# Gated MLP of a decoder trunk: chunk 3 moved from plain products to seven block products, and the opening's splits reordered

## The chip, the cores and the metric

The kernel runs on one core of a Trainium2 chip. The metric is device time in microseconds of one execution; lower is better. A core has TensorE (PE, matrix products into PSUM), VectorE (DVE), ScalarE (ACT), GpSimd (POOL) and SyncE (SP), which issues most loads. POOL issues the transfers that add into their destination.

## The reference, cut to what matters

Two layers. Layer 0 begins with a mixer of a gated recurrence and pooling, layer 1 with a convolution module; both then have cross-attention and a gated MLP, and a norm ends the trunk. All is float32, with 512 tokens of width 1024. The MLP:

```python
def conv_ffn(x, norm, w_up, dw_w, dw_b, w_down):
    h = rms_norm(x, norm) @ w_up                       # 1024 -> 2 x 3072
    g = causal_dwconv(h[..., :D_FF], dw_w, dw_b)       # width 3
    u = h[..., D_FF:]
    return (jax.nn.gelu(g) * u) @ w_down
```

## The kernel before, in words

Activations lie transposed: partitions hold channels, the 512 columns are tokens. Every operand of a product is split into a high half (a copy rounded to fp32r, on ScalarE) and a low half (the rest, by a subtraction on VectorE), and a product is three matmuls, high-high, high-low and low-high (`mm3`, lines 183 to 187).

The 3072 channels of the gate and of the value branch are 24 chunks of 128 each (`CF`). Chunk c of the gate and chunk c of the value make a chunk pair. A layer's `ffn` (line 813) does the pairs in two ways.

The first four (`GC` = 4) are plain, in `opening` (line 938). `start(i)` (944) is one product of 128 weight columns with all 512 tokens: 8 blocks x 3 = 24 matmuls of 512 columns. Even i is a gate, odd i a value. `fetch(i)` (951) loads the piece of weights for it, 512 KB, and makes its high half; `w[-1].low()` makes the low half. `gate(c)` (955) is a generator in four steps: multiply by the norm's factor and scale for the convolution; two shifted multiply-adds; GELU; multiply by the norm's factor again. `values(c)` (971) multiplies by the value and makes the high half of the result, `close(c)` (976) the low half.

The other pairs are units (`unit(c)`, 867). Gate and value chunk, each in two halves of input channels, are seen as a 2 x 2 block matrix, the tokens' halves as another, and the product is made with seven block products in place of eight, after Strassen and Winograd: seven times 4 blocks x 3 = 12 matmuls of 256 columns, and seven additions of half width (line 170) plus one copy (880). The weights are four blocks (a11 and a12 are the gate chunk's two halves, `z` and a22 the value chunk's) and four sums of them (s1 to s4). A sum is not computed on an engine: a transfer on POOL's queue adds one block to another in SBUF, in place, issued right behind the low half that was the last reader of the old content (`Blocks.low`, line 797 and on):

```python
            if name == "a11":
                G.dma_start(self.r, self.z, accum_op=ALU.add)     # line 803, gives s3
            elif name == "a22" and not self.ring:
                G.dma_start(self.z, self.a22, accum_op=ALU.add)   # line 805, gives s1
            elif name == "s3":
                G.dma_start(self.r, self.a22, accum_op=ALU.add)   # line 807, gives s2
            elif name == "s2":
                G.dma_start(self.r, self.a12, accum_op=ALU.add)   # line 811, gives s4
```

So a11, s3, s2 and s4 of one pair are a chain through one buffer, and a22 and s1 another; each split (high at line 793, low at 800) has to wait for the transfer in front of it. The tokens' sums are made by `Seven.sums(k)` for k = 0 to 3 (727); the last, `sums(3)`, stands in the opening.

A unit c also has work for its neighbours: the splits of pair c + 1 and the first of pair c + 2, and two down products (`Down`, 816) of 12 matmuls of 512 columns each, of which the second runs over into the next unit's additions. Down products begin with chunk 4, when the first group of four chunks is complete. In a unit the order of products is a11, a12, s2, s3, then the first down product, s1, s4, a22, then the second.

Within `tc.manual_schedule(engines=ORDERED)` the queues of PE, ACT, DVE and POOL run in program order, so a waiting instruction holds all behind it. SP's order is chosen by the scheduler: a load goes out when its buffer is free. There are 3 buffers for raw weights, 4 each for their wide high and low halves, 4 for the small blocks a12 and a22, and 5 PSUM banks for the products.

Of the kernel before, what the change touches and what calls it, by code (L numbers as in the profile page):

```python
# [15 lines left out]
P = 128  # L16
# [8 lines left out]
CF = D_FF // P  # L25
NG = 6
GC = CF // NG
EPS = 1e-6
AHEAD = 100
PAIRED = (0, 4, 1, 5, 2, 6, 3, 7)  # L30
# [30 lines left out]
def trunk(ctx: ExitStack, tc: tile.TileContext, I: dict, out: list):  # L61
# [751 lines left out]
    def ffn(layer, norm, nxt, seven):  # L813
# [19 lines left out]
                if self.g == NG - 1:  # L833
                    nxt.feed(n)

        pairs = {c: Blocks(I["wpair"][layer * (CF - GC) + c - GC]) for c in range(GC, CF)}
        downs = {c: Down(*divmod(c - GC, GC)) for c in range(GC, CF + GC)}

        def high(c, name):
            if c in pairs:  # L840
                pairs[c].high(name)

        def low(c, name):
            if c in pairs:
                pairs[c].low(name)

        def gating(c, f, g, ps, u3):
# [19 lines left out]
        def unit(c):  # L867

            nonlocal left, due

            def m(j, block):
                return seven.product(main_ps()[:, :M], pairs[c].w[block], j)

            f, g, u, v = tmp_f(), tmp_f(), tmp_f(), tmp_f()
            m1, u2, u3, u4 = u[:, :M], u[:, M:], v[:, :M], v[:, M:]
            ps = m(seven.B11, "a11")
            next(left, None)
            A.activation(m1, ps, AF.Copy)  # L880
            high(c + 1, "s3")
            high(c + 1, "a22")
            if due:
                due()
            next(left, None)

            ps = m(seven.B21, "a12")
            low(c + 1, "s3")
            low(c + 1, "a22")
            add(g[:, :M], ps, m1)  # L890
            next(left, None)

            ps = m(seven.T2, "s2")
            high(c, "s4")
            high(c + 2, "a11")
            high(c + 1, "a12")
            add(u2, ps, m1)
            low(c, "s4")

            ps = m(seven.T3, "s3")  # L900
            low(c + 2, "a11")
            low(c + 1, "a12")
            add(u3, ps, u2)
            if c in downs:
                due = downs[c].out(0, aux_ps())
            if c + 1 in downs:
                downs[c + 1].w.high()
            if c + 3 in pairs:
                pairs[c + 3].load()
            if c + 2 in pairs:  # L910
                pairs[c + 2].load_second()
            if c + 1 in downs:
                downs[c + 1].w.low()
            if c + 2 in downs and c + 2 <= CF:
                downs[c + 2].load()
            if due:
                due()

            ps = m(seven.T1, "s1")
            high(c + 1, "s2")  # L920
            add(u4, ps, u2)
            add(f[:, M:], ps, u3)

            ps = m(seven.B22, "s4")
            low(c + 1, "s2")
            high(c + 1, "s1")
            add(g[:, M:], ps, u4)

            ps = m(seven.T4, "a22")
            left = gating(c, f, g, ps, u3)  # L930
            next(left)
            low(c + 1, "s1")
            next(left)
            if c in downs:
                due = downs[c].out(1, aux_ps())


        def opening():


            nonlocal left, due
            norm.r, ps, y = None, {}, [None] * GC

            def start(i):

                ps[i] = main_ps()
                x = w.pop(0)
                for k in range(C):
                    mm3(ps[i], blk(x, k * P), norm.x[k], k == 0, k == C - 1)

            def fetch(i):
                w.append(Piece(I["wup"][(layer * 2 + i % 2) * GC + i // 2]))
                w[-1].high()

            def gate(c):
                g = tmp_f()
                V.tensor_tensor(g, ps.pop(2 * c), norm.r, op=ALU.mult)
                y[c] = tmp_f()
                dw = lambda j: col("f_dw_w", (layer * 3 + j) * CF + c)
                A.activation(y[c], g, AF.Identity, scale=dw(2), bias=col("f_dw_b", layer * CF + c))  # L960
                yield
                for s in (1, 2):
                    V.scalar_tensor_tensor(
                        y[c][:, s:], g[:, : T - s], dw(2 - s), y[c][:, s:], op0=ALU.mult, op1=ALU.add
                    )
                yield
                A.activation(y[c], y[c], AF.Gelu_apprx_tanh)
                yield
                V.tensor_tensor(y[c], y[c], norm.r, op=ALU.mult)

            def values(c):
                V.tensor_tensor(y[c], ps.pop(2 * c + 1), y[c], op=ALU.mult)
                ys[c] = act_r(), act_r()
                A.activation(ys[c][0], y[c], AF.Copy)

            def close(c):
                V.tensor_tensor(ys[c][1], y[c], ys[c][0].bitcast(F32), op=ALU.subtract)

            ss = split(norm.ss)
            start(0)  # L980
            fetch(2)
            w[-1].low()
            for name in ("a11", "a22", "a12"):
                high(first, name)
                low(first, name)
            norm.r = scale_of(mean_of(ss))
            Norm.due = None

            start(1)
            fetch(3)  # L990
            w[-1].low()
            g = gate(0)
            next(g)
            high(first, "s3")
            high(first, "s1")
            next(g)
            low(first, "s3")
            next(g)
            low(first, "s1")
            next(g, None)  # L1000

            start(2)
            fetch(4)
            values(0)
            w[-1].low()
            close(0)

            start(3)
            fetch(5)
            w[-1].low()  # L1010
            g = gate(1)
            next(g)
            high(first, "s2")
            next(g)
            low(first, "s2")
            next(g)
            next(g, None)

            start(4)
            fetch(6)  # L1020
            w[-1].low()
            values(1)
            t = seven.sums(3)
            next(t)
            close(1)
            next(t, None)

            start(5)
            fetch(7)
            w[-1].low()  # L1030
            g = gate(2)
            next(g)
            next(g)
            next(g)
            next(g, None)

            start(6)
            pairs[second].load()
            pairs[second].load_second()
            downs[first].load()  # L1040
            values(2)
            close(2)
            high(second, "a11")

            start(7)
            downs[first].w.high()
            g = gate(3)
            next(g)
            low(second, "a11")
            next(g)  # L1050
            downs[first].w.low()
            next(g)
            downs[second].load()
            pairs[second + 1].load()
            next(g, None)

            def rest():
                values(3)
                yield
                close(3)  # L1060

            left, due = rest(), None

        left, due = None, None
        first, second = GC, GC + 1
        with tc.high_priority(AHEAD):
            w = [Piece(I["wup"][(layer * 2 + k) * GC]) for k in range(2)]
            for x in w:
                x.high()
                x.low()  # L1070
# [2 lines left out]
            pairs[first].load_second()  # L1073
        with tc.manual_schedule(engines=ORDERED):
            opening()
            for c in range(GC, CF):
                unit(c)
            due()
            for _ in left:
                pass  # L1080
# [572 lines left out]
    with tc.manual_schedule(engines=ORDERED | {mybir.EngineType.SP}):  # L1653
# [20 lines left out]
        ps = [[mm_ps(), mm_ps()] for _ in range(2)]  # L1674
# [28 lines left out]
        w = [Piece(I["wk"][0])]  # L1703
# [61 lines left out]
def _cols(w):  # L1765

    k, n = w.shape
    return w.reshape(k // P, P, n // P, P).transpose(2, 1, 0, 3).reshape(n // P, P, k)
# [9 lines left out]
def _fours(g, v):  # L1778

    return np.concatenate([g[:, :, :T], v[:, :, :T], v[:, :, T:], g[:, :, T:]], axis=2)  # L1780


def _layout(inputs):
    a = {k: np.asarray(v) for k, v in inputs.items()}
    params = []
    w = np.concatenate([np.zeros((1, D), np.float32), a["c_dw_w"][0]])[::-1].reshape(8, 4, C, 4, 32)[:, ::-1]
    a["c_dw_w"] = a["c_dw_w"][:, :TAPS]
    a["c_dw_pe"] = w.transpose(2, 0, 3, 4, 1)
    for name, width in _PARAMS:
# [4 lines left out]
    up = a["f_w_up"]  # L1794
# [17 lines left out]
        "wk": np.concatenate([_cols(w) for w in a["xa_wk"]]),  # L1812
        "wv": wv,
        "wo": np.concatenate([_cols(w) for w in a["xa_wo"]]),
        "wup": np.concatenate([_cols(w[:, at : at + GC * P]) for w in up for at in (0, CF * P)]),
        "wpair": np.concatenate([_fours(w[GC:CF], w[CF + GC :]) for w in map(_cols, up)]),
        "final_norm": np.broadcast_to(a["final_norm"], (P, D)),
        "wdown": np.concatenate([_pairs(w, GC).reshape(-1, P, D) for w in a["f_w_down"]]),
    }
# [19 lines left out]
```

## Time and profile before

| | before |
|---|---|
| median of 3 runs | 1432.36 us |
| lowest, highest | 1431.59, 1434.14 us |
| the profiled execution | 1434.17 us |
| its span | 1432.3 us |
| PE, DVE, ACT, POOL busy | 99%, 82%, 56%, 21% |
| opening of the MLP, layer 0, start(0) to the first unit | 356.1 to 400.1 us |
| one unit with its two down products | 15.55 us |

The profile is of one execution. The busy share counts an engine's instructions, recorded lengths united; matmuls are pipelined, so a matmul's recorded length is longer than the step to the next. Lines of the profile name the engine, the kernel's line, the tiles written and read, the count, and in a timeline the start in us from the beginning of the span, with the idle time in front and what ended it in brackets.

### The profile page before, as it was taken

The numbers are of one execution on the slowest core, as the hardware profiler recorded it, in microseconds if no ns is written. First come the engines' busy times: TensorE is split into PE (matmuls) and PEld (weight loads), VectorE is DVE, ScalarE is ACT, GpSimd is POOL, SyncE is SP. The second block draws the span as 40 slices with busy tenths as digits, with TensorE's granted clock in tenths as the row PEclk, the third lists the DMA queues.
The fourth block names the chain that finished last, engine by engine and source line by source line (L and its number), as shares of the span: only waits on it lengthen the run. The fifth ranks groups of instructions, "written<-read, shape, count | busy, mean of one in ns | idle before, by whom it ended". The sixth has DMA issues, their size and how long they took to land.

```text
span 1432.3 us, 22644 instructions
## 1 busy us (share of the span) xinstructions
PE 1419.6 (99%) x8504; PEld 1257.3 (88%) x8504; DVE 1176.7 (82%) x1955; ACT 798.2 (56%) x1321; POOL 304.4 (21%) x317
## 2 busy tenths in 40 slices
PE   9999999999999999999999999999999999999997
PEld 7888888998899999999988777899889999999997
DVE  6987776778788888888888997978778888888885
ACT  7678754666544444544565547767655444444434
POOL 0001310200021221222008992010001222222201
PEclk9999999999999999999999999999999999999999
DMA  8523232542557777777432464345244876787741
GB/s 292 198 81 99 93 118 81 118 111 89 158 136 169 162 182 165 163 173 173 136 123 89 118 167 143 107 87 147 87 129 121 178 179 157 171 184 159 162 126 59
DMA packets 77517, 200.11 MB, mean 140 GB/s; under 512 B 8672, under 2 KB 9952, under 8 KB 77408
## 3 DMA queue, kind: packets, MB, share of 16 engines
q1 hardware_dynamic: 50624, 150.15, 33.6%
q0 software_dynamic: 26496, 48.25, 20.5%
q8 instruction: 67, 1.10, 0.3%
q14 instruction: 42, 0.34, 0.1%
q10 hardware_dynamic: 288, 0.27, 0.1%
HBM read 145.16 MB, written 2.10 MB: 103 GB/s over the span
## 4 chain that ended last, share of the span: by engine, by line
PE 91%; DVE 3%; POOL 2%; DMA 2%; ACT 1%; issue 1%; SPq 0%; POOLq 0%; ACTq 0%; DVEq 0%
PE mm L186 22%; PE mm L185 22%; PE mm L187 22%; PE aux L185 7%; PE aux L186 7%; PE aux L187 7%; PE mm L456 2%; DMA raw<-in_wv 1%; DVE wlo L166 1%; POOL actf L1443 1%; PE aux L529 0%; ACT whi L165 0%; POOL act L166 0%; POOL tmp L1264 0%; DMA raw<-in_win 0%
## 5 line engine op out<-in xcount | busy, mean ns | idle before, releaser
L186 PE MATMUL mm<-act,whi 128*128 128x512 f32 (+2 forms) x1093 | 385.1, 352 | 0.6 <-DVE act L180 0.5
L185 PE MATMUL mm<-act,whi 128*128 128x512 f32 (+2 forms) x1093 | 384.6, 353 | 0.1
L187 PE MATMUL mm<-act,wlo 128*128 128x512 f32 (+2 forms) x1093 | 384.6, 352 | 0.0
L186 PEld LDWEIGHTS mm<-act,whi 128*128 128x128 f32 x1093 | 206.6, 189 | 30.3 <-DVE act L166 1.0
L185 PEld LDWEIGHTS mm<-act,whi 128*128 128x128 f32 x1093 | 206.4, 189 | 30.0 <-ACT tmp L1442 0.8
L187 PEld LDWEIGHTS mm<-act,wlo 128*128 128x128 f32 x1093 | 206.6, 189 | 27.0
L793 ACT ACTIVATE bigr<-raw 128x512 fp32r<-128x512 f32 x160 | 100.7, 630 | 156.7 <-DMA raw<-wa 64.3
L187 PE MATMUL mm<-bigr,bigr 128*128 128x256 f32 x640 | 181.1, 283 | 0.0
L186 PE MATMUL mm<-bigr,bigr 128*128 128x256 f32 x640 | 181.1, 283 | 0.0
L185 PE MATMUL mm<-bigr,bigr 128*128 128x256 f32 x640 | 180.9, 283 | 0.0
L170 DVE TENSOR_TENSOR tmp<-mm,tmp 128x256 f32<-128x256 f32 x322 | 131.2, 420 | 34.7 <-PE mm L187 28.3
L185 PE MATMUL aux<-act,whi 128*128 128x512 f32 x399 | 156.3, 392 | 0.0
L186 PE MATMUL aux<-act,whi 128*128 128x512 f32 x399 | 156.2, 391 | 0.0
L187 PE MATMUL aux<-act,wlo 128*128 128x512 f32 x399 | 155.2, 389 | 0.0
L165 ACT ACTIVATE whi<-raw 128x1024 fp32r<-128x1024 f32 (+1 forms) x95 | 96.6, 1021 | 85.5 <-PE mm L186 44.5
L800 DVE TENSOR_TENSOR bigr<-raw,bigr 128x512 fp32r<-128x512 f32 x160 | 110.0, 688 | 32.4 <-ACT bigr L793 30.4
L186 PEld LDWEIGHTS mm<-bigr,bigr 128*128 128x128 f32 x640 | 122.7, 192 | 1.6
L185 PEld LDWEIGHTS mm<-bigr,bigr 128*128 128x128 f32 x640 | 122.7, 192 | 1.6
L187 PEld LDWEIGHTS mm<-bigr,bigr 128*128 128x128 f32 x640 | 122.7, 192 | 0.0
L803 POOL DMA_DIRECT2D raw<-raw x46 | 39.8, 866 | 350.8 <-DVE wlo L800 303.9
L166 DVE TENSOR_TENSOR wlo<-raw,whi 128x1024 fp32r<-128x1024 f32 (+1 forms) x75 | 90.7, 1212 | 19.7 <-ACT whi L165 19.5
L807 POOL DMA_DIRECT2D raw<-wa x46 | 39.7, 864 | 303.2 <-DVE bigr L800 253.6
(341 smaller groups left out, 3013.4 us busy)
## 6 DMA issues: line engine op xcount, KB each, us to landing
raw<-wa POOLq DMA_DIRECT2D x138, 256.0 KB, 4.4
big<-in_wdown SPq DMA_DIRECT2D x42, 512.0 KB, 6.7
wa<-in_wpair SPq DMA_DIRECT2D x80, 256.0 KB, 3.4
raw<-in_wpair SPq DMA_DIRECT2D x40, 512.0 KB, 5.7
raw<-in_pw SPq DMA_DIRECT2D x24, 512.0 KB, 3.5
raw<-raw POOLq DMA_DIRECT2D x46, 256.0 KB, 7.3
raw<-in_win SPq DMA_DIRECT2D x20, 512.0 KB, 3.4
raw<-in_wk SPq DMA_DIRECT2D x16, 512.0 KB, 3.7
```

The lines of the kernel that those rows point to most:

```text
L165: A.activation(hi, src, AF.Copy)
L166: fetched[1] = (eng or V).tensor_tensor(lo, src, hi.bitcast(F32), op=ALU.subtract)
L170: V.tensor_tensor(out, a, b, op=ALU.add)
L185: PE.matmul(ps, wh, xh, start=first, stop=False)
L186: PE.matmul(ps, wh, xl, start=False, stop=False)
L187: PE.matmul(ps, wl, xh, start=False, stop=last)
L456: PE.matmul(p, m[j], x, start=k == 0 and j == 0 and x is hi, stop=k == C - 1 and x is lo)
L793: A.activation(self.w[name][0], self.block(name), AF.Copy)
L800: V.tensor_tensor(lo, self.block(name), hi.bitcast(F32), op=ALU.subtract)
L803: G.dma_start(self.r, self.z, accum_op=ALU.add)
L807: G.dma_start(self.r, self.a22, accum_op=ALU.add)
L1443: G.tensor_tensor(z[:, s:], z[:, s:], f[:, s:], op=ALU.add)
```

## The change

`PLAIN = 3` takes the place of `GC` wherever the number of plain pairs is meant, so that chunks 0 to 2 stay plain and chunk 3 becomes the first unit, in both layers. `GC` stays the number of chunks in a down group; unit 3 has no down products. The opening then holds start(0) to start(5). Its splits are put in another order: each split of a block sum (s3, s1, s2) of the first unit's pair comes some steps behind the transfer that makes the sum. The splits of a11, a22 and a12 of the second pair, chunk 4, are also made in the opening; the set `early` keeps the unit from making them again. `sums(3)` moves from start(4) to start(3), and the low half of a piece often behind the first step of a gate. The host's layout of the two weight arrays follows.

```diff
+PLAIN = 3
...
-        pairs = {c: Blocks(I["wpair"][layer * (CF - GC) + c - GC]) for c in range(GC, CF)}
+        pairs = {c: Blocks(I["wpair"][layer * (CF - PLAIN) + c - PLAIN]) for c in range(PLAIN, CF)}
...
+        early = set()
+
         def high(c, name):
-            if c in pairs:
+            if c in pairs and (c, name) not in early:
                 pairs[c].high(name)
...
-            if c + 1 in downs:
+            if c >= GC and c + 1 in downs:
                 downs[c + 1].w.high()
...
             start(1)
             fetch(3)
-            w[-1].low()
             g = gate(0)
             next(g)
+            w[-1].low()
             high(first, "s3")
-            high(first, "s1")
+            fetch(4)
+            next(g)
             next(g)
             low(first, "s3")
-            next(g)
-            low(first, "s1")
+            w[-1].low()
             next(g, None)
 
             start(2)
-            fetch(4)
             values(0)
-            w[-1].low()
+            fetch(5)
             close(0)
+            high(first, "s1")
 
             start(3)
-            fetch(5)
-            w[-1].low()
+            downs[GC].load()
+            pairs[second].load_second()
             g = gate(1)
             next(g)
-            high(first, "s2")
+            w[-1].low()
+            low(first, "s1")
+            pairs[second].load()
             next(g)
-            low(first, "s2")
-            next(g)
-            next(g, None)
-
-            start(4)
-            fetch(6)
-            w[-1].low()
-            values(1)
             t = seven.sums(3)
             next(t)
+            next(g)
+            next(t, None)
+            high(second, "a11")
+            next(g, None)
+
+            start(4)
+            values(1)
+            low(second, "a11")
+            early.add((second, "a11"))
+            high(first, "s2")
             close(1)
-            next(t, None)
+            low(first, "s2")
 
             start(5)
-            fetch(7)
-            w[-1].low()
+            downs[GC].w.high()
             g = gate(2)
             next(g)
+            high(second, "a22")
+            downs[GC].w.low()
             next(g)
             next(g)
+            high(second, "a12")
+            low(second, "a22")
             next(g, None)
-
-            start(6)
...
-            start(7)
...
+            low(second, "a12")
+            early.update(((second, "a22"), (second, "a12")))
             pairs[second + 1].load()
-            next(g, None)
...
-        first, second = GC, GC + 1
+        first, second = PLAIN, PLAIN + 1
...
-            for c in range(GC, CF):
+            for c in range(PLAIN, CF):
                 unit(c)
```

More of the change, by code (lines that the diff above doesn't have):

```diff
@@ L834, in sum @@
                     nxt.feed(n)
-        pairs = {c: Blocks(I["wpair"][layer * (CF - GC) + c - GC]) for c in range(GC, CF)}
+        pairs = {c: Blocks(I["wpair"][layer * (CF - PLAIN) + c - PLAIN]) for c in range(PLAIN, CF)}
         downs = {c: Down(*divmod(c - GC, GC)) for c in range(GC, CF + GC)}
+        early = set()
         def high(c, name):
-            if c in pairs:
+            if c in pairs and (c, name) not in early:
                 pairs[c].high(name)
         def low(c, name):
-            if c in pairs:
+            if c in pairs and (c, name) not in early:
                 pairs[c].low(name)
@@ L911, in unit @@
                 pairs[c + 2].load_second()
-            if c + 1 in downs:
+            if c >= GC and c + 1 in downs:
                 downs[c + 1].w.low()
@@ L941, in opening @@
             nonlocal left, due
-            norm.r, ps, y = None, {}, [None] * GC
+            norm.r, ps, y = None, {}, [None] * PLAIN
             def start(i):
@@ L951, in fetch @@
             def fetch(i):
-                w.append(Piece(I["wup"][(layer * 2 + i % 2) * GC + i // 2]))
+                w.append(Piece(I["wup"][(layer * 2 + i % 2) * PLAIN + i // 2]))
                 w[-1].high()
@@ L1008, in opening @@
             start(3)
-            fetch(5)
-            w[-1].low()
+            downs[GC].load()
+            pairs[second].load_second()
             g = gate(1)
             next(g)
-            high(first, "s2")
+            w[-1].low()
+            low(first, "s1")
+            pairs[second].load()
             next(g)
-            low(first, "s2")
+            t = seven.sums(3)
+            next(t)
             next(g)
+            next(t, None)
+            high(second, "a11")
             next(g, None)
@@ L1019, in opening @@
             start(4)
-            fetch(6)
-            w[-1].low()
             values(1)
-            t = seven.sums(3)
-            next(t)
+            low(second, "a11")
+            early.add((second, "a11"))
+            high(first, "s2")
             close(1)
-            next(t, None)
+            low(first, "s2")
             start(5)
-            fetch(7)
-            w[-1].low()
+            downs[GC].w.high()
             g = gate(2)
             next(g)
+            high(second, "a22")
@@ L1033, in opening @@
+            downs[GC].w.low()
             next(g)
             next(g)
+            high(second, "a12")
+            low(second, "a22")
             next(g, None)
-            start(6)
[L1038 to L1043, printed above, removed]
-            start(7)
-            downs[first].w.high()
-            g = gate(3)
-            next(g)
-            low(second, "a11")
@@ L1050, in opening @@
[L1050 to L1053, printed above, removed]
+            low(second, "a12")
+            early.update(((second, "a22"), (second, "a12")))
             pairs[second + 1].load()
-            next(g, None)
             def rest():
-                values(3)
+                values(2)
                 yield
-                close(3)
+                close(2)
             left, due = rest(), None
         left, due = None, None
-        first, second = GC, GC + 1
+        first, second = PLAIN, PLAIN + 1
@@ L1066, in ffn @@
         with tc.high_priority(AHEAD):
-            w = [Piece(I["wup"][(layer * 2 + k) * GC]) for k in range(2)]
+            w = [Piece(I["wup"][(layer * 2 + k) * PLAIN]) for k in range(2)]
             for x in w:
@@ L1814, in _layout @@
         "wo": np.concatenate([_cols(w) for w in a["xa_wo"]]),
-        "wup": np.concatenate([_cols(w[:, at : at + GC * P]) for w in up for at in (0, CF * P)]),
-        "wpair": np.concatenate([_fours(w[GC:CF], w[CF + GC :]) for w in map(_cols, up)]),
+        "wup": np.concatenate([_cols(w[:, at : at + PLAIN * P]) for w in up for at in (0, CF * P)]),
+        "wpair": np.concatenate([_fours(w[PLAIN:CF], w[CF + PLAIN :]) for w in map(_cols, up)]),
         "final_norm": np.broadcast_to(a["final_norm"], (P, D)),
```

## The prediction

> **What bounds the kernel now.** I read the page's head and chain first, then the waits of TensorE, then stretches of the gated MLP.
>
> ```profile
> span 1432.3 us, 22644 instructions
> PE 1419.6 (99%) x8504; PEld 1257.3 (88%) x8504; DVE 1176.7 (82%) x1955; ACT 798.2 (56%) x1321; POOL 304.4 (21%) x317
> PE 91%; DVE 3%; POOL 2%; DMA 2%; ACT 1%; issue 1%; SPq 0%; POOLq 0%; ACTq 0%; DVEq 0%
> ```
>
> TensorE is 99% busy and carries 91% of the chain. A busy share can hide pauses, since matmuls overlap, so the waits are the better witness:
>
> ```profile
> PE stat L297 <- DVE actf L1458: 1.8, 1, 1.8
> PE mm L456 <- ACT whi L165: 1.7, 2, 1.5
> PE stat L138 <- POOL onesf L127: 1.0, 1, 1.0
> PE mm L186 <- DVE act L180: 0.5, 1, 0.5
> PE aux L348 <- DVE act L327: 0.2, 1, 0.2
> ```
>
> These are all its waits, 5.2 us, and none belongs to the MLP's opening or units (their matmuls stand on lines 185 to 187; the one wait there, behind line 180, is a projection's operand). So in the MLP TensorE never waits, and the time is the number of matmuls times their spacing. The reader should price a matmul by starts, not by its recorded length:
>
> ```profile
> 362.00 0.40 PE L185 MATMUL mm<-act,whi 128*128 128x512 f32 x1
> ...
> 400.10 0.28 PE L185 MATMUL mm<-act,whi 128*128 128x256 f32 x1
> ...
> 402.97 0.28 PE L185 MATMUL mm<-bigr,bigr 128*128 128x256 f32 x1
> ...
> 405.85 0.40 PE L185 MATMUL aux<-act,whi 128*128 128x512 f32 x1
> ```
>
> From 362.00 to 400.10 stand the plain products start(1) to start(7): 7 x 24 = 168 matmuls of 512 columns in 38.10 us, 0.2268 us each. From 402.97 to 405.85 stand two block products of the first unit, 24 matmuls of 256 columns in 2.88 us, 0.120 us each.
>
> ```profile
> core 0: us, PE busy (x) PEld busy (x) DVE busy (x) ACT busy (x) POOL busy (x), PEclk, DMA share, GB/s
> 362.00:400.10 38.10, 38.10 (x170) 31.54 (x169) 29.57 (x42) 21.11 (x30) 3.94 (x5) 1.00 0.53 152
> 400.10:415.65 15.55, 15.55 (x109) 14.57 (x108) 13.38 (x23) 7.07 (x12) 3.86 (x5) 1.00 0.68 148
> 415.65:431.20 15.55, 15.55 (x109) 14.58 (x108) 15.02 (x26) 7.07 (x12) 3.47 (x4) 1.00 0.77 179
> ...
> 1049.65:1087.75 38.10, 38.10 (x170) 31.54 (x168) 29.57 (x42) 21.00 (x30) 3.96 (x5) 1.00 0.54 152
> ```
>
> The clock is granted in full (1.00), and layer 1's opening (last row) takes the same 38.10 us. The second engine is VectorE (DVE): 29.57 of 38.10 us in the opening, up to 15.02 of 15.55 us in a unit.
>
> **The change, part by part.**
>
> *TensorE.* Chunk 3 leaves the opening: 2 products x 24 = 48 matmuls of 512 columns, 48 x 0.2268 = 10.89 us. It comes back as a unit of 7 products x 12 = 84 matmuls of 256 columns, 84 x 0.120 = 10.08 us. It has no down products beside it, since those begin at chunk 4. Gain 0.81 us a layer, 1.61 us in both, all of it on the path as long as TensorE still never waits.
>
> The Trainium skill, page "TensorE: Matmul & The Clock Gate", section "Back-to-back issue gap", speaks against the change: it says that in a stream of weight loads and matmuls both set the spacing, about 81 ns at 128 columns and 131 ns at 512. Between them 256 columns would be an estimated 98 ns, and 84 x 98 is 1.9 us more than 48 x 131, so 3.9 us slower in all; this trace, with 120 and 227 ns, does not agree, and the sum goes by the trace.
>
> *VectorE and ScalarE.* Prices from the groups with shapes kept apart:
>
> ```profile
> L800 DVE TENSOR_TENSOR bigr<-raw,bigr 128x512 fp32r<-128x512 f32 x160 | 110.0, 688 | 32.4 <-ACT bigr L793 30.4
> L793 ACT ACTIVATE bigr<-raw 128x512 fp32r<-128x512 f32 x160 | 100.7, 630 | 156.7 <-DMA raw<-wa 64.3 <-DVE wlo L202 53.1 <-PE mm L187 36.1
> L202 DVE TENSOR_TENSOR wlo<-raw,whi 128x1024 fp32r<-128x1024 f32 x32 | 39.0, 1219 | 2.8 <-ACT whi L199 2.5
> L199 ACT ACTIVATE whi<-raw 128x1024 fp32r<-128x1024 f32 x32 | 33.7, 1052 | 8.4 <-PE aux L186 4.4 <-PE mm L186 2.2 <-DMA raw<-in_wk 1.8
> L170 DVE TENSOR_TENSOR tmp<-mm,tmp 128x256 f32<-128x256 f32 x322 | 131.2, 420 | 34.7 <-PE mm L187 28.3 <-ACT bigr L793 3.2
> L880 ACT ACTIVATE tmp<-mm 128x256 f32<-128x256 f32 x40 | 15.3, 383 | 21.5 <-PE mm L187 21.4
> ```
>
> A layer gains seven low halves (7 x 0.69) and seven half-width adds (7 x 0.42) on VectorE and loses two wide low halves (2 x 1.22): +5.3 us. ScalarE gains 7 x 0.63 + 0.38 and loses 2 x 1.05: +2.7 us. Convolution, gate and output split are the same instructions in both forms. This hides only under TensorE: start(1) to start(5) and the new unit last 5 x 24 x 0.2268 + 10.08 = 37.3 us, and VectorE then needs 29.6 + 5.3 = 34.9 of them, 94%. ScalarE needs 21.1 + 2.7 = 23.8. It fits in sum; if it didn't, the excess would come through one to one. So the question is whether the work comes in time.
>
> *The order, worked through for layer 0.* In time of the profile, the unit for chunk 3 starts at 400.10 - 10.89 = 389.21. Its sixth product, the first that needs a split made late (s4), starts five products later: 389.21 + 5 x 1.44 = 396.4. VectorE has its operands from the end of the reciprocal on. Instructions follow each other closer than they last:
>
> ```profile
> 364.41 3.35 DVE L307 RECIPROCAL r<-tmp 128x512 f32<-128x512 f32 x1 [0.53 <-ACT tmp L305]
> ...
> 392.94 1.54 DVE L963 SCALAR_TENSOR_TENSOR tmp<-tmp,par,tmp 128x511 f32<-128x511 f32 x2 [0.89 <-ACT tmp L960]
> ...
> 405.17 0.69 DVE L800 TENSOR_TENSOR bigr<-raw,bigr 128x512 fp32r<-128x512 f32 x1
> 405.78 0.69 DVE L800 TENSOR_TENSOR bigr<-wa,bigr 128x512 fp32r<-128x512 f32 x1
> ```
>
> A 512-column operation takes 405.78 - 405.17 = 0.61 of the queue; the same 0.08 off the recorded lengths, I estimate 1.1 for a wide one (1.22), 0.35 for a half one (0.42) and 1.5 for a pair of taps (1.54). From 367.8 to that s4 split stand 12 plain operations of gates, values and closings, 8 block lows, 4 wide lows, 3 tap pairs, 8 of the pooled sums and 2 adds: 20 x 0.61 + 4 x 1.1 + 3 x 1.5 + 10 x 0.35 = 24.6 us, so 392.4 at the earliest. Queue waits add to that: in each of three gates about 0.9 behind the scaling of y (the row at 392.94), some shadowed by a block split put there. Followed through instruction by instruction, they come to about 3 us and s4 is ready at about 395.3, 1.1 us early. That margin is the narrow point; before, the same split was later but needed later:
>
> ```profile
> 407.05 0.68 DVE L800 TENSOR_TENSOR bigr<-raw,bigr 128x512 fp32r<-128x512 f32 x1
> 410.03 0.28 PE L185 MATMUL mm<-act,bigr 128*128 128x256 f32 x1
> ```
>
> There the low half ended at 407.73 and the product came at 410.03, 2.3 us later, since 12 down matmuls stood between.
>
> *The transfers.* GpSimd (POOL) gets four more adding transfers a layer; SP's two 512 KB pieces become one of 512 KB and two of 256 KB, the same bytes. SP's order isn't written by hand. The small blocks of the next pair go out long before (the row at 294.92), and chunk 4's large block when the fourth piece's buffer is free, near 373; a median 5.7 us later it is there, and a11 is split near 382:
>
> ```profile
> raw<-in_wpair SPq DMA_DIRECT2D x40, 512.0 KB, 5.7
> ...
> 294.92 0.33 SPq L773 DMA_DIRECT2D wa<-in_wpair  x1
> ...
> L807 POOL DMA_DIRECT2D raw<-wa x46: 857/862/885, 251.8 to 1371.4; - x46
> DMA to landing us min/median/max: 3.2/3.4/5.1
> ...
> L811 POOL DMA_DIRECT2D raw<-wa x46: 857/862/887, 256.8 to 1379.8; - x46
> DMA to landing us min/median/max: 3.3/4.6/6.0
> ```
>
> For chunk 3 each transfer is issued 5 to 8 us ahead of the split that reads it. That is the second half of the change: before, too, no TensorE wait came of those splits, so reordering them is worth 0. The wait that the change does make is for chunk 4. Its s3 low half ends at about 394.0, deep in the short unit; the transfer behind it is issued near 394.3 and lands 3.2 to 5.1 us later (L807), at 397.5 to 399.4; s2 is split 1.3 us (0.63 + 0.69) after, at 398.8 to 400.7. TensorE asks for it as the third product of the next unit, at 399.29 + 2 x 1.44 = 402.2: 1.5 us spare at the worst landing. Behind the waiting copy on ScalarE stand the s1 copy, gate 3's scaling and GELU and the m1 copy; on VectorE behind the low half the add of g's second half, which frees a PSUM bank, and gate 3. So the waiting shows first as lateness there. The next transfer (L811, 3.3 to 6.0 us) and s4's split end between 404 and 408.5; TensorE asks at 399.29 + 5 x 1.44 + 12 x 0.2268 = 409.2. I take 0 us of stall, as the rows near it have none. The upper bound is VectorE's queue waits at twice my 3 us, which makes s4 1.9 us late a layer; below nothing it cannot go, because TensorE has no wait there to lose.
>
> **Sum.** The profiled execution took 1434.17 us, its span 1432.3 and 1.9 us around it; minus 1.61 that is 1432.6. It lies 1.8 us above the median of the three runs, 1432.36, so I carry the difference over: 1432.36 - 1.61 = 1430.75, written 1430.8.
>
> **Rivals.**
> *Late s4, gain eaten.* VectorE reaches chunk 3's s4 (or chunk 4's) later than my walk by more than its 1.1 us margin, and TensorE waits by the excess; for it speaks 94% of VectorE, against it the 15.02 of 15.55 us at which a unit runs without a wait. At half as much waiting again (4.5 us) s4 is 0.4 us late, at twice 1.9: 1430.75 + 0.8 to 1430.75 + 3.8, so 1431.5 to 1434.5.
> *Slower: the s3 transfer of chunk 4 lands late.* In the new short unit there are no down products to cover it. It decides when the landing takes over 402.2 - 394.3 - 1.3 = 6.6 us; L807's worst is 5.1, but those of line 803, one of which stands right behind it in the queue, have been slower:
>
> ```profile
> L803 POOL DMA_DIRECT2D raw<-raw x46: 852/862/1010, 241.2 to 1359.0; - x46
> DMA to landing us min/median/max: 3.3/7.3/9.0
> ```
>
> At 9.0 us TensorE waits 2.4 us for s2, and s4's split (another transfer behind it) some 0.6 more: +3.0 - 0.8 = 2.2 a layer, 1432.36 + 4.4 = 1436.8.
> *Slower: the weight loads set the pace.* 84 loads replace 48.
>
> ```profile
> L185 PEld LDWEIGHTS mm<-bigr,bigr 128*128 128x128 f32 x640 | 122.7, 192 | 1.6
> ```
>
> If each took its 0.192 us alone, 84 x 0.192 = 16.1 us, 5.2 more than 10.89 a layer: 1442.8. The rows at 402.97 and 405.85 have the same loads at 0.120, so this is nearly excluded. The page of the Trainium skill named above states the rule by which it would be so.
> *The change does more.* 1.61 us is all that the matmuls can give, and no TensorE wait is there to go; only scatter reaches below 1429.5.
>
> **How the numbers follow.** A run of this kernel can tell about 0.2% (2.9 us) from no change, so the computed gain of 0.11% lies inside. Forecast, 1429.5 to 1431.5 with scatter: 0.57. Late s4, up to 1435.2 with scatter: 0.27. Late transfer 0.10 and weight loads 0.01, above 1435.2. More than computed: 0.05. So within 0.2% 0.84, slower 0.11, faster 0.05. The range takes the forecast from its lower scatter to the upper bound of the late s4: 1429.5 to 1434.5, which leaves out about 0.18.
>
> **What would show it.** Right: in each layer's opening six plain products, then 84 matmuls at 0.120 us in 10.1 us, the first down product 0.8 us earlier counted from start(1), and no TensorE wait for lines 170, 793 or 800. Wrong: TensorE pauses before the sixth product of chunk 3's unit (the first rival), or before the third or sixth of chunk 4's, with ScalarE ended by the transfer of line 807 (the second), or a spacing above 0.130 us, which is 48 x 0.2268 / 84 (the third).

## The result and the profile after

| | before | after |
|---|---|---|
| median of 6 runs beside each other | 1432.89 us | 1440.01 us |
| lowest, highest | 1431.59, 1434.35 us | 1439.28, 1441.66 us |
| ratio after to before, 95% interval | | 1.0053 [1.0042, 1.0064] |
| the profiled execution, its span | 1434.17, 1432.3 us | 1441.66, 1439.9 us |

The changed kernel is 7.1 us slower (0.5%), outside the range. The head of its page and its shares of the chain (in after, the matmuls, the weights' splits and the adding transfers stand one line lower in the file, so their line numbers are one higher than in before; further down the shift is larger):

```profile
span 1439.9 us, 22868 instructions
...
PE 1422.3 (99%) x8576; PEld 1261.3 (88%) x8576; DVE 1184.9 (82%) x1979; ACT 800.8 (56%) x1333; POOL 310.8 (22%) x325
...
PE 82%; DVE 5%; DMA 4%; issue 4%; ACT 2%; POOL 2%; POOLq 0%; SPq 0%; DVEq 0%; ACTq 0%
```

TensorE still reads 99% busy, but its share of the chain fell from 91% to 82%: here the busy share hides what the chain shows. The waits of TensorE in after name the place:

```profile
PE aux L186 <- ACT act L866: 3.5, 2, 1.8
PE aux L187 <- DVE act L868: 1.5, 2, 0.7
...
PE mm L188 <- DVE bigr L801: 0.4, 2, 0.2
```

Each occurs twice, once a layer; the numbers are the total, the times and the longest one in us. `aux` is a down product; lines 866 and 868 make the high and low half of a unit's output. Before, the MLP's units had no wait at all. And two of the longest single pieces of after's chain point to the cause, once a layer:

```profile
393.62 7.24 DMA raw<-wa
...
1084.38 7.15 DMA raw<-wa
```

Both are the transfer of line 808 (807 in before) for chunk 4, the one whose landing the prediction put at 3.2 to 5.1 us. (The same list has in each layer a piece of "issue" of 7.6 us, on POOL's queue about 17 us earlier, in the opening. It didn't set the transfer's start: POOL's queue waited for the low half of s3 on VectorE, which ended at 393.32.) Now the stretches of the opening and the new unit, with the columns that the prediction's windows had:

```profile
core 0: us, PE busy (x) PEld busy (x) DVE busy (x) ACT busy (x) POOL busy (x), PEclk, DMA share, GB/s
361.35:388.57 27.22, 27.22 (x122) 22.53 (x120) 25.21 (x37) 17.39 (x26) 4.86 (x6) 1.00 0.61 154
388.57:398.65 10.08, 10.08 (x86) 10.08 (x85) 6.75 (x13) 3.61 (x7) 2.02 (x3) 1.00 0.72 163
398.65:414.15 15.50, 12.80 (x90) 11.32 (x89) 11.59 (x20) 7.57 (x13) 3.47 (x4) 1.00 0.72 163
...
1095.00:1110.10 15.10, 12.62 (x68) 11.01 (x67) 13.72 (x24) 6.94 (x12) 3.48 (x4) 0.89 0.79 176
```

The five plain products take 27.22 us (120 x 0.2268) and the new unit 10.08 us (84 x 0.120), both as computed. What is lost lies behind them, in chunk 4's unit (third row), and in layer 1 the clock falls as well (0.89 in the last row).

Counted from start(1), all down products from chunk 5's unit on are late by a constant amount: 2.92 us in layer 0, 4.33 in layer 1. In layer 0 that is the gain of 0.81 against 3.72 us of pauses, counted by the starts of the matmuls; layer 1 has 3.62 us of pauses and 1.52 at the low clock. Three terms stand outside the layers' MLPs: 0.75 us more from the start of the last down product to the end (36.14 before, 36.89 after), an earlier start(1) of layer 0 (361.35 in place of 362.00, -0.65), and 0.19 between the layers. The sum is 7.5 us, the difference of the two spans.

**The chain, step by step, in layer 0.** ScalarE's queue in after, then VectorE's, then the down product of chunk 4 on TensorE:

```profile
400.94 1.15 ACT L794 ACTIVATE bigr<-raw 128x512 fp32r<-128x512 f32 x2 [7.31 <-DMA raw<-wa]
403.39 0.81 ACT L855 ACTIVATE tmp<-tmp,par 128x512 f32<-128x512 f32 x1 [1.30 <-DVE tmp L854]
406.56 0.63 ACT L862 ACTIVATE tmp<-tmp 128x512 f32<-128x512 f32 x1 [2.35 <-DVE tmp L860]
...
408.40 0.62 ACT L866 ACTIVATE act<-tmp 128x512 fp32r<-128x512 f32 x1
```

```profile
401.61 0.69 DVE L801 TENSOR_TENSOR bigr<-raw,bigr 128x512 fp32r<-128x512 f32 x1 [4.89 <-ACT bigr L794]
...
402.67 0.69 DVE L854 TENSOR_TENSOR tmp<-tmp,r 128x512 f32<-128x512 f32 x1
...
409.56 0.68 DVE L868 TENSOR_TENSOR act<-tmp,act 128x512 fp32r<-128x512 f32 x1
```

```profile
406.93 0.39 PE L188 MATMUL aux<-act,wlo 128*128 128x512 f32 x1
409.07 0.50 PE L186 MATMUL aux<-act,whi 128*128 128x512 f32 x1 [1.75 <-ACT act L866]
410.30 0.51 PE L187 MATMUL aux<-act,whi 128*128 128x512 f32 x1 [0.72 <-DVE act L868]
```

ScalarE stands still for 7.31 us, VectorE for 4.89, both on s2 of chunk 4. Behind them in program order stands the whole gate of chunk 3: scaling (854, 855), taps (860), GELU (862), output split (866, 868). The first three quarters of chunk 4's down product read chunks 0 to 2 and run; the last quarter reads chunk 3 and comes at 409.07 in place of 407.16 (406.93 + 0.227), then waits again for the low half. So the largest pause isn't at the product that reads s2 (0.7 us), but at one that reads something else behind it in the queues.

Why the landing took 7.24 us: the transfer queues in after between its issue and its landing, and, for the same transfer with nothing beside it, those of before (the one from 372.81). Columns are packets, MB, and the packets' time as a share of the 16 engines:

```profile
q1 hardware_dynamic: 288, 1.05, 53.0%
q0 software_dynamic: 260, 0.49, 37.6%
...
raw<-wa POOLq DMA_DIRECT2D x1, 256.0 KB, 7.2
raw<-raw POOLq DMA_DIRECT2D x1, 256.0 KB, 6.7
```

```profile
q0 software_dynamic: 144, 0.26, 44.9%
issues: line engine op xcount, KB each, median us to landing
raw<-wa POOLq DMA_DIRECT2D x1, 256.0 KB, 3.2
```

q0 carries POOL's adding transfers, q1 the loads. Alone, the engines move 0.26 MB of adds and the transfer lands in 3.2 us; in after, two 512 KB loads (down weights, issued at 393.07, and chunk 6's blocks, at 394.61) take 53% of the engines' time in that stretch. A second adding transfer stands there too (last row: chunk 5's a11, issued at 395.48), so the loads are not the only suspect; loads_later, below, decides between the two.

### The profile page after: what moved, and what is told of

It reads as the page before. It is cut to its first block, busy times and chain, and to the rows that moved or that the text cites. A ratio compares the mean times of both kernels' runs of the same rounds, so it can differ in the third digit from the quotient of the medians.

```text
span 1439.9 us, 22868 instructions
## 1 busy us (share of the span) xinstructions
PE 1422.3 (99%) x8576; PEld 1261.3 (88%) x8576; DVE 1184.9 (82%) x1979; ACT 800.8 (56%) x1333; POOL 310.8 (22%) x325
## 4 chain that ended last, share of the span: by engine, by line
PE 82%; DVE 5%; DMA 4%; issue 4%; ACT 2%; POOL 2%; POOLq 0%; SPq 0%; DVEq 0%; ACTq 0%
PE mm L187 20%; PE mm L188 20%; PE mm L186 20%; PE aux L187 7%; PE aux L186 7%; PE aux L188 7%; PE mm L457 2%; DMA raw<-in_wv 1%; DMA raw<-wa 1%; DVE wlo L167 1%; DMA raw<-in_wpair 1%; POOL actf L1436 1%; ACT whi L166 1%; PE aux L530 0%; DVE r L308 0%
## 5 line engine op out<-in xcount | busy, mean ns | idle before, releaser
L187 PE MATMUL mm<-act,whi 128*128 128x512 f32 (+2 forms) x1077 | 377.2, 350 | 0.6 <-DVE act L181 0.5
L186 PE MATMUL mm<-act,whi 128*128 128x512 f32 (+2 forms) x1077 | 376.7, 351 | 0.0
L188 PE MATMUL mm<-act,wlo 128*128 128x512 f32 (+2 forms) x1077 | 376.7, 350 | 0.0
L187 PEld LDWEIGHTS mm<-act,whi 128*128 128x128 f32 x1077 | 203.7, 189 | 29.2 <-DVE act L167 1.0
L186 PEld LDWEIGHTS mm<-act,whi 128*128 128x128 f32 x1077 | 203.4, 189 | 28.8 <-ACT tmp L1435 0.8
L188 PEld LDWEIGHTS mm<-act,wlo 128*128 128x128 f32 x1077 | 203.6, 189 | 25.5
L794 ACT ACTIVATE bigr<-raw 128x512 fp32r<-128x512 f32 x168 | 105.2, 628 | 163.3 <-DMA raw<-wa 65.6
L188 PE MATMUL mm<-bigr,bigr 128*128 128x256 f32 x672 | 190.8, 284 | 0.4 <-DVE bigr L801 0.4
L187 PE MATMUL mm<-bigr,bigr 128*128 128x256 f32 x672 | 190.4, 283 | 0.0
L186 PE MATMUL mm<-bigr,bigr 128*128 128x256 f32 x672 | 190.4, 283 | 0.0
L171 DVE TENSOR_TENSOR tmp<-mm,tmp 128x256 f32<-128x256 f32 x336 | 136.5, 418 | 36.5 <-PE mm L188 30.5
L801 DVE TENSOR_TENSOR bigr<-raw,bigr 128x512 fp32r<-128x512 f32 x168 | 115.5, 688 | 40.9 <-ACT bigr L794 38.7
L186 PEld LDWEIGHTS mm<-bigr,bigr 128*128 128x128 f32 x672 | 129.1, 192 | 1.8 <-ACT bigr L794 0.2
L187 PEld LDWEIGHTS mm<-bigr,bigr 128*128 128x128 f32 x672 | 129.1, 192 | 1.6
L188 PEld LDWEIGHTS mm<-bigr,bigr 128*128 128x128 f32 x672 | 129.1, 192 | 0.9 <-DVE bigr L801 0.9
```

Of the source, the lines that this page charges most:

```text
L171: V.tensor_tensor(out, a, b, op=ALU.add)
L186: PE.matmul(ps, wh, xh, start=first, stop=False)
L187: PE.matmul(ps, wh, xl, start=False, stop=False)
L188: PE.matmul(ps, wl, xh, start=False, stop=last)
L794: A.activation(self.w[name][0], self.block(name), AF.Copy)
L801: V.tensor_tensor(lo, self.block(name), hi.bitcast(F32), op=ALU.subtract)
```

## The experiments

Theory: chunk 4's s3 transfer lands late because two loads share the transfer engines, and chunk 3's gate, queued behind the splits that wait for it, reaches the down product late. Rivals: the new order of the splits costs the time; the down product is late for lack of VectorE time; the landing is long for a reason other than the loads, such as the adding transfer behind it. Each edit is shown against after, and that of before_pad against before; `...` stands for lines left out. The first four kernels ran beside 27 runs of before with a median of 1433.03 us, the last three beside 27 with 1432.52.

**order_only**: chunk 3 still plain as in before, with the change's order of the first pair's splits, of the wide low halves and of `sums(3)` in the opening. Of the second pair only a11 is split there, as in before. The rest of the edit puts start(6), start(7) and gate(3) back.

```diff
-PLAIN = 3
+PLAIN = 4
...
```

> All four plain pairs kept, chunk 4 still the first unit; only the order of the opening's splits, of the wide low halves and of the last pooled sums is the changed one. Theory (the loss sits in chunk 3's unit, where the s3 transfer of chunk 4 lands 7 us after its start and ScalarE and VectorE stand still behind it): the order alone costs nothing, 1432.9 us within 0.5, no wait of TensorE in the MLP. Rival (the new order makes VectorE late): TensorE waits 1 us or more in chunk 4's unit, over 1434.5.

Measured 1433.48 us (1431.83 to 1434.74, 10 runs), ratio 1.0004 [0.9995, 1.0013], 0.1 us above the expected 1432.9 within 0.5. No wait of TensorE in the MLP, every unit at before's distance from start(1) to 0.01 us. The reordering alone neither gains nor costs anything that these runs can tell.

**seven_only**: the seven products for chunk 3, the splits in before's order, of chunk 4 only a11 split in the opening. The cut shows the second part; the reordering is left out.

```diff
...
-            high(second, "a22")
...
-            high(second, "a12")
-            low(second, "a22")
...
-            low(second, "a12")
...
```

> Chunk 3 by seven products, but the splits of the opening in the order of before, and of chunk 4 only a11 split in the opening. Theory: the s3 transfer again starts in the short unit, the waits come again or larger, since a22's transfer now stands beside it: TensorE waits 3 to 6 us a layer, 1437 to 1443 us. Rival (the new order brought the loss): no wait, 1431.3 us.

Measured 1442.42 us (1441.70 to 1442.67, 4 runs), ratio 1.0066 [1.0051, 1.0081]. Its waits of TensorE:

```profile
PE aux L186 <- ACT act L866: 3.1, 2, 2.0
PE mm L188 <- DVE bigr L801: 2.1, 2, 1.1
PE aux L187 <- DVE act L868: 1.4, 2, 0.7
PE mm L186 <- ACT bigr L794: 1.1, 2, 0.5
```

The down product's waits are there as in after, and the late s4 of chunk 3 (first rival of the prediction; the two waits of `mm`) comes on top: about 2.1 us a layer, counted by starts. So the loss comes with the block products, and the new order takes part of it away.

**gate_first**: in chunk 3's unit alone, the split of chunk 4's s2 goes behind chunk 3's gate. The transfers and loads stay.

```diff
-            high(c + 1, "s2")
+            if c > PLAIN:
+                high(c + 1, "s2")
...
+            if c == PLAIN:
+                high(c + 1, "s2")
+                low(c + 1, "s2")
```

> As changed, but in chunk 3's unit alone the split of chunk 4's s2 stands behind chunk 3's gate, so that nothing of the gate queues behind the wait for the transfer. Theory (the pause at the first down product is chunk 3's output, held up in the two queues): the waits for lines 866 and 868 go (2.9 us a layer), some 0.7 us a layer for s2 itself stays: 1432.9 - 1.6 + 1.4 = 1432.7 us, 1432 to 1433.6, and no fall of the granted clock. Rival (the transfer's landing alone sets the end): TensorE's pause only moves to s2 and s4, total over 1438.

Measured 1434.78 us (1432.72 to 1437.69, 11 runs), ratio 1.0013 [1.0004, 1.0021]; expected were 1432 to 1433.6. In its trace the s3 transfer of chunk 4 still takes 7.08 us (392.63 to 399.70), and yet there is one wait of TensorE a layer left in the units, for s2 itself:

```profile
PE mm L188 <- DVE bigr L801: 0.7, 2, 0.4
```

ScalarE now does the scaling at 397.58, while the transfer is under way, and the output's high half at 402.59, 42.25 us behind start(1) (360.34) in place of 47.05 in after:

```profile
397.58 0.82 ACT L855 ACTIVATE tmp<-tmp,par 128x512 f32<-128x512 f32 x1 [3.43 <-DVE tmp L854]
399.79 0.63 ACT L794 ACTIVATE bigr<-raw 128x512 fp32r<-128x512 f32 x1 [1.39 <-DMA raw<-wa]
400.75 0.63 ACT L862 ACTIVATE tmp<-tmp 128x512 f32<-128x512 f32 x1 [0.33 <-DVE tmp L860]
```

With the late landing kept, taking the gate from behind it removes the 3 us at the down product, and in this trace the clock stays full in both layers. VectorE does the same work here, so lack of VectorE time was not the cause of these 3 us. Counted from start(1), the down products stand 0.15 us earlier than in before; yet its median lies 1.75 us above before's and its runs are widely spread. The 0.74 us at the end (below) is part of that. The rest stays open: the profiled execution was one of the fastest (1432.98 us), and two runs of 1435.8 us had granted clocks of 0.997 and 0.999, so a fall of the clock alone doesn't explain it.

**s3_early**: chunk 4's s3 is split in the opening, so that its transfer goes out earlier.

```diff
             next(g)
+            high(second, "s3")
             high(second, "a12")
             low(second, "a22")
+            low(second, "s3")
...
-            early.update(((second, "a22"), (second, "a12")))
+            early.update(((second, "a22"), (second, "a12"), (second, "s3")))
```

> As changed, but chunk 4's s3 is split in the opening, behind chunk 2's GELU, so that its transfer starts near 390.5 in place of 393.6, before the loads of 393 to 395. Theory (the late landing is the cause): it lands before 396, no wait of TensorE in either MLP, all 0.81 us a layer are kept: 1432.9 - 1.6 = 1431.3 us, 1430.3 to 1432.2. Rival (VectorE is too full in the opening): the split put there delays the gates, TensorE waits over 1 us a layer, over 1433.3.

Measured 1432.97 us (1431.56 to 1434.28, 11 runs), ratio 0.9997 [0.9989, 1.0006]. The transfer goes out at 391.62 and lands at 396.08 (4.46 us, beside one load of 256 KB; SP sends the two loads of 512 KB only at 396.54 and 397.01). No wait of TensorE is left in the units, and the first down product stands 0.80 us closer to start(1) than in before, in both layers: the whole computed gain, for the first time (0.14 of it is lost again in a later unit of layer 0). But the time isn't the expected 1.6 us better, since the end is 0.86 us longer and the layers stand 0.5 us further apart.

**loads_later**: the two 512 KB loads of chunk 3's unit go out on ScalarE's queue behind chunk 4's s2 copy, so that the transfer runs alone. The order of gate and splits is that of after.

```diff
...
-            if c + 3 in pairs:
+            if c + 3 in pairs and c > PLAIN:
...
-            if c + 2 in downs and c + 2 <= CF:
+            if c + 2 in downs and c + 2 <= CF and c > PLAIN:
...
+            if c == PLAIN:
+                pairs[c + 3].load(A)
+                downs[c + 2].load(A)
```

> As changed, but the two 512 KB loads that went out during chunk 3's unit (down weights of chunk 5, large block of chunk 6) go out behind chunk 4's s2 split. Theory (those loads share the transfer engines with chunk 4's s3 transfer and double its time): it lands 3.3 to 4.5 us after its start in place of 7.2, s2 is split before TensorE asks, the pauses of 3.7 us a layer go: about 1432 us, 1431 to 1433. Rival (the adding transfer of chunk 5's a11 behind it in POOL's queue slows it): it still takes over 6 us and TensorE pauses as before, about 1440 us.

Measured 1432.81 us (1432.08 to 1434.65, 10 runs), ratio 1.0003 [0.9994, 1.0012]. The transfer queues of this kernel over the landing:

```profile
q0 software_dynamic: 145, 0.26, 46.7%
issues: line engine op xcount, KB each, median us to landing
raw<-wa POOLq DMA_DIRECT2D x1, 256.0 KB, 3.3
raw<-raw POOLq DMA_DIRECT2D x1, 256.0 KB, 3.5
```

3.30 us in place of 7.24 (3.24 in place of 7.15 in layer 1), with gate and splits as in after; the waits at the down product are gone. The adding transfer of chunk 5's a11 is issued 1.87 us behind, as in after (last row), so without the loads it doesn't stretch the landing. So the loads made the landing long. A later unit loses 0.55 us in layer 0 and 0.2 in layer 1. In layer 0 the wait is at chunk 5's s4, whose pair had its s3 transfer (issued at 404.49) stretched to 8.89 us beside SP's next loads (404.61 to 406.70); that this is the reason was argued from the trace, not tested. This run also gives the price of lateness: the landing is 3.94 us sooner than in after, and the low half of chunk 3's output ends 3.94 us sooner (44.95 us behind start(1), after 48.89). It comes through one to one.

**s3_early_pad** and **before_pad** ask what makes the end longer. The five kernels with three plain pairs measured so far needed 36.75 to 37.00 us from the start of the last down product to the end of the span, before and order_only 36.14 and 36.16. In after, two instruction fetches (queue 14) fall into the stretch from the last store's issue to the end, in before none. First after, then before (the last row is the landing of the last store on SP's queue):

```profile
q14 instruction: 2, 0.02, 1.6%
...
last<-big SPq DMA_DIRECT2D x1, 256.0 KB, 3.5
```

```profile
q1 hardware_dynamic: 387, 0.61, 43.5%
q10 hardware_dynamic: 144, 0.26, 18.3%
issues: line engine op xcount, KB each, median us to landing
last<-big SPq DMA_DIRECT2D x1, 256.0 KB, 2.5
```

Both kernels only get small instructions (fills of one column on POOL at the start, tiny loads on SP between the layers) that shift where the instruction streams of these two engines cross a fetch. s3_early_pad has 40 and 24 of them on top of s3_early, before_pad 16 and 6 on top of before.

```diff
...
+    for t in range(40):
+        G.memset(spare[:, :1], 0.0)
...
+    for t in range(24):
+        nc.sync.dma_start(more[:, 2 * t : 2 * t + 2], I["params"][:, :2])
```

> The version with chunk 4's s3 split in the opening, and with 40 single-column fills on POOL at the start and 24 tiny loads on SP between the layers, which compute nothing. Theory (the two 8 KB fetches of instructions that the shorter opening's extra instructions moved into the last 4 us hold up the last stores by 0.75 us): the fetches leave the tail, the last down product of layer 1 to the end takes 36.15 us again in place of 36.9, total 1432.9 - 1.5 = 1431.4 us, 1430.3 to 1432.3. Rival (the tail is longer for another reason): the tail stays 36.9 us.

> The kernel before, with 16 single-column fills on POOL and 6 tiny loads on SP added, which compute nothing and bring both queues near the changed kernel's lengths. Theory of the instruction fetch: one or two fetches of 8 KB now fall into the last 4 us and the tail lasts 36.6 to 36.9 us in place of 36.15; the total 0.5 to 0.8 us above before. Rival: the tail keeps its 36.15 us.

s3_early_pad took 1431.21 us (1430.85 to 1433.16, 11 runs), ratio 0.9995 [0.9986, 1.0004]; before_pad 1433.47 (1432.45 to 1434.71, 10 runs), ratio 1.0007 [0.9998, 1.0016]. From the last down product to the end s3_early_pad needs 35.85 us, before_pad 37.04 (expected 36.6 to 36.9). The stretch from the last store's issue to the end, in s3_early_pad and then in before_pad:

```profile
q1 hardware_dynamic: 318, 0.50, 36.8%
q10 hardware_dynamic: 144, 0.26, 18.9%
issues: line engine op xcount, KB each, median us to landing
last<-big SPq DMA_DIRECT2D x1, 256.0 KB, 2.4
```

```profile
q14 instruction: 2, 0.02, 1.4%
...
last<-big SPq DMA_DIRECT2D x1, 256.0 KB, 2.9
```

Without a fetch there the end is short, with two it is long, in a kernel with the change and in one without. All nine traces agree: from the last store's issue to the end the three without a fetch need 3.61 to 3.89 us, the six with two fetches 4.51 to 4.79, and from the last down product to that issue all nine need the same, 32.24 to 32.30 us. The longer end is therefore not the block products' own; instructions added elsewhere bring it or take it away. How a fetch delays the end was not separated from the extra instructions themselves. s3_early_pad also has its -0.80 us undisturbed in both layers. Its median is the lowest of all and 1.3 us under that of before beside it, but its interval contains 1: no version was shown to beat before. In its profile part of the lead comes from elsewhere, too: beyond the gain, its layers stand 1.06 us closer together than before's (those of before_pad 0.59 us), which no run explains.

## Why the prediction was wrong

*The matmuls: right.* 27.22 and 10.08 us, and 0.80 us saved a layer as soon as nothing waits (s3_early).

*VectorE and chunk 3's s4: right.* VectorE was busy 25.21 of 27.22 us in the five plain products. With the new unit that makes 31.96 us (25.21 + 6.75), where the sum had 34.9; how much of the rest slipped behind the late transfer was not separated. The s4 low half ended at 394.58 (393.90 + 0.68 in VectorE's timeline), the product came at 395.77: 1.2 us spare, forecast 1.1. This was the narrow point of the walk, and it held. seven_only shows that it does fail with the old order.

*The reordering: right alone (order_only), not in company.* It is worth nothing to before and, with the early splits of a22 and a12, about 2.4 us to a kernel with the seven products (1442.42 less 1440.01).

*Chunk 4's s3 transfer, the step that failed.* The issue was forecast well: 394.3 in before's time, less the 0.65 us by which after starts earlier, is 393.65, measured 393.62. Also the time at which TensorE asks for s2, 402.2, less the same 0.65, is 401.55; it came to 401.52 (401.40 + 0.12). Wrong was "lands 3.2 to 5.1 us later (L807)". The row's extremes were taken from other places of the kernel, without asking what SP would send at the same moment; it sent two 512 KB loads, and the landing took 7.24. Loads_later shows the cause. The rival's rule, decided at 6.6 us, gives 0.64 us of waiting for s2, and 0.70 was measured.

*"So the waiting shows first as lateness there", the reader that was missed.* The text listed gate 3 behind the waiting copy and stopped. Gate 3 ends in chunk 3's output, and chunk 4's first down product reads it about 2 us after it begins. Before, chunk 3 was plain and its output split stood free of any transfer. In loads_later the low half is ready at 44.95 us, the matmul that reads it starts at 45.35: 0.40 us spare at a landing of 3.30. So by this run the landing decides from 3.7 us on, not from 6.6, and the stall should be 7.24 - 3.70 = 3.54 us; the pauses sum to 3.72. Even L807's worst of 5.1 would by that have cost an estimated 1.4 us a layer, more than the gain. "I take 0 us of stall" fell here. The second rival had the right transfer, with too small a chance. That its price of 3.0 us a layer lies near the measured 3.72 is luck: it stood for a landing of 9.0 us, with s2 and s4 as readers. At the measured 7.24 its rule gives the 0.64 above; the other 3.0 us were lost at a reader that it doesn't name, and chunk 4's s4 never waited.

*Not in the sum:* the clock in layer 1 (1.5 us) and the end (0.75 us).

## What to carry to other kernels

Where a change adds a wait to an in-order queue, follow what stands behind the waiting instruction to its last reader on the bottleneck engine, and compute the spare time there: at a landing of 3.3 us it was 0.4 us, where the direct reader had 3.3 (6.6 - 3.3). A transfer's landing time belongs to its moment: look at which loads are issued within a few us of it, since 3.3 us alone became 7.2 beside 1 MB of loads. A gain of 1.6 us in all is hardly larger than what the end of the kernel varied by from version to version (35.85 to 37.04 us), so it shows clearly only when it is counted from a mark inside the layer.

## What the runs showed of the hardware

**The clock fell to half after pauses, in one layer of two.** After equal pauses at the down product (1.9 and 1.0 us), layer 1 ran at half the clock for 3.4 us and layer 0 didn't. After's windows behind the pause of layer 1:

```profile
1102.14:1105.50 3.36, 3.36 (x18) 3.36 (x17) 3.36 (x7) 0.69 (x2) 0.86 (x1) 0.50 1.03 224
1105.60:1110.00 4.40, 4.40 (x28) 3.95 (x28) 3.91 (x8) 1.34 (x2) 0.88 (x1) 1.00 0.74 150
```

The granted clock reads 0.50 from 1102.14 to 1105.50, and matmuls of 256 columns started every 0.213 us in place of 0.120. The fall comes about 1 us after the pause is over. The Trainium skill, page "TensorE: Matmul & The Clock Gate", section "Part 1: The HAM clock gate (the "warmup" mystery)", says that activity is watched in free-running windows of 3413 ns. The length of the slow stretch agrees with that; a window that lies differently to the pause would also explain why layer 0 was spared, but no run here tested it. The fall needed no whole window of idling: the longest single wait in front of it was 1.75 us. seven_only shows a fall at the same place, also in layer 1 alone (a granted clock of 0.86 from 1100 to 1112).

**Loads stretch adding transfers.** An adding transfer of 256 KB took 3.2 to 3.3 us with no load beside it and 7.1 to 7.2 beside two 512 KB loads. In loads_later those loads left on ScalarE's queue at 396.46 and 396.84, after the landing at 396.35, so what helped was the later time; whether ScalarE's queue matters was not tested. The Trainium skill, page "DMA: Bandwidth & Descriptors", section "Issuing engines are not separate DMA queues", says that transfers of all issuing engines run on the same 16 DMA engines and interleave; these landings agree.

**Instruction fetches at the very end went with a longer end.** Two fetches of queue 14 behind the last store's issue went with 4.51 to 4.79 us from there to the end, none with 3.61 to 3.89 (six and three traces). The Trainium skill, page "Runtime: NRT & Kernel Launch", section "Instruction fetch mechanics", calls the fetch mostly hidden; at the end of this kernel the time does not seem to stay hidden, as far as these traces can tell.
